# A whole network's instructions ordered by the language's timing model, with a new loading order for its input

## The chip, the core and the metric

The kernel runs on one core of a Trainium2 chip. The metric is the device time of one execution in microseconds. The kernel before takes 1856.32 us, the median of three runs between 1855.94 and 1859.72 us. The engines are called by their short names: PE multiplies matrices, DVE (VectorE) and ACT (ScalarE) work element by element on 128 partitions, POOL (GpSimd) helps out, SP issues DMAs.

## The reference

The input is 512 tokens of 1024 channels. The network has a first part of two layers and a second part of one layer. Layer A of the first part is what most of this text is about: attention in which every query attends only to the 128 best keys, chosen by a score of its own.

```python
def dsa_mixer(x, cos, sin, w_in, w_o):
    top_k = min(IDX_TOPK_MAX, L // 4)                     # 128
    q, k, v, iq, ik, iw = jnp.split(x @ w_in, A_SPLITS, axis=-1)
    ...                                                   # rotary on q, k, iq, ik
    s = einsum('bqhd,bsd->bqhs', iq_b, ik) * IDX_DIM ** -0.5
    score = einsum('bqh,bqhs->bqs', iw_b, relu(s))        # 8 index heads
    score = where(causal, score, -inf)
    _, sel = lax.top_k(score, top_k)
    p = softmax(logits of q against the selected keys)    # 16 heads, 4 kv heads
    return einsum(p, v_sel) @ w_o

def first_block(x, ...):      # layer A, then layer B
    h = layer_norm(ALPHA * h + mixer(h)); h = layer_norm(ALPHA * h + relu(h @ w_up)**2 @ w_down)

def second_block(x, c, ...):  # attention and a two-way mLSTM side by side, then a gated MLP
```

Layer B's mixer is a gated linear attention (GLA): a state per head is carried over chunks of 64 tokens; its output is normalised per head, multiplied by a gate silu(r), and projected.

## The kernel before

**Arithmetic and tiles.** Products in f32 are made from two rounded parts: `hi` (L88, on ACT) copies a tile to the type fp32r, `lo` (L85, on DVE) subtracts that copy from the original, and a product x·w becomes three PE products, hi·hi, lo·hi and hi·lo. Weights go through the same split: a piece of a weight arrives by DMA as `wr`, ACT makes `wh`, DVE makes `wl` (128x1024 at a time in most places). The 512 tokens are four tiles of 128, numbered 0 to 3. `x_tok` is the input with tokens on partitions, `xT_hi` and `xT_lo` are the transposed parts. `transpose_half` makes them: four PE transposes of 128x128 into one PSUM bank `ps_t`, then hi and lo.

**PSUM.** There are eight banks: three named `ps_a` (projections), two `ps_t` (transposes), two `ps_s` (scores), one `ps_o` (attention output).

**Layer A** (`layer_a`). It projects iq, then k and ik, and then runs the steps of the list `ORDER_A` (L22): S3 is the score of tile 3, V the projection of the values, Q0 and Q1 those of the queries (two groups of 8 heads), B3 the search of the best keys of tile 3, A30 the attention of tile 3 with head group 0, O the output projection. Tile 0 needs no search: all its causal keys are selected. A score (L508 to L526) is, for each of 8 index heads, two PE products into `ps_s`, a relu on ACT (`rl`), and one DVE instruction that adds into `sc`; tile t has 128·(t+1) keys, so `sc1` is 128x256, `sc2` 128x384, `sc3` 128x512. A search (L528 to L535) is sixteen rounds on DVE of MAX8 (the eight largest of a row), MATCH_VALUE_LOAD and MATCH_REPLACE8 (strike them out), and a last TENSOR_SCALAR (L535), which turns `sc` into the bias that the softmax adds. The attention of a tile and group (`softmax_pv`) is, for each of 8 heads, two products into `ps_s`, a DVE instruction that adds the bias and takes the row minimum (L428, `prob,mn<-ps_s,sc`), an exp on ACT (L434), a reciprocal on DVE, a normalisation on DVE or ACT, PE transposes (L443) and an ACT copy (L448), and then products with v into `ps_o`.

**GLA.** After the chunk recurrence, each head's output `gy` is copied from PSUM (L847, DVE), squared and summed (L851, ACT), a square root is taken over all sixteen sums at once (L866, ACT), then a reciprocal (L867, DVE); L883 multiplies by the gate, and `transpose_half` feeds the output projection.

**What sets the order.** The functions write instructions in program order, with pools of buffers; `urgent` gives loads and weight splits an earlier place. From this the language's scheduler makes one list per engine. An engine runs its list in order.

## Time and profile before

| | |
|---|---|
| median of three runs | 1856.32 us (1855.94 to 1859.72) |
| the profiled execution, its own time | 1859.66 us |
| its span in the profile | 1857.9 us |
| PE busy in the span | 1815.5 us |
| DVE busy | 1440.5 us |
| ACT busy | 912.3 us |

Layer A with its output projection and norm takes the first 240 us or so, the first MLP follows, the GLA lies around 600 to 800 us, the second MLP until 1165 us, the second part's mixer until about 1510 us, and its MLP to the end. In the rows below, a line such as "88.09 0.88 DVE L533 MAX8 m<-sc 128x8 f32<-128x256 f32 x2" gives the start of a run of alike instructions, its length to the end of the last one, the engine, the line in the kernel, the operation, output and inputs, and the count. The end of one instruction overlaps the start of the next by about 0.1 us, so the cadence is read from starts.

### The profile page before, as it was taken

The numbers are of one execution on the slowest core, as the hardware profiler recorded it, in microseconds if no ns is written. First come the engines' busy times: TensorE is split into PE (matmuls) and PEld (weight loads), VectorE is DVE, ScalarE is ACT, GpSimd is POOL, SyncE is SP. The second block draws the span as 40 slices with busy tenths as digits, with TensorE's granted clock in tenths as the row PEclk, the third lists the DMA queues.
The fourth block names the chain that finished last, engine by engine and source line by source line (L and its number), as shares of the span: only waits on it lengthen the run. The fifth ranks groups of instructions, "written<-read, shape, count | busy, mean of one in ns | idle before, by whom it ended". The sixth has DMA issues, their size and how long they took to land.

```text
span 1857.9 us, 26802 instructions
## 1 busy us (share of the span) xinstructions
PE 1815.5 (98%) x10564; PEld 1532.8 (83%) x10564; DVE 1440.5 (78%) x2467; ACT 912.3 (49%) x1600; POOL 19.0 (1%) x46
## 2 busy tenths in 40 slices
PE   8999999999999999999999999999999899999997
PEld 7865698988888888889888888777566689999996
DVE  5998589878678587468988777877876787788877
ACT  5568644444443544334544444445677445344334
POOL 0010000000000100000000000000000000000000
PEclk9999999999999999999999999999999999999999
DMA  4231244634324222126454323422112122333232
GB/s 143 91 68 52 67 139 158 207 117 148 103 91 134 61 69 69 68 91 188 140 180 140 113 92 111 139 73 81 46 41 69 45 91 68 114 114 114 79 104 91
DMA packets 127161, 190.80 MB, mean 103 GB/s; under 512 B 9279, under 2 KB 77835, under 8 KB 127036
## 3 DMA queue, kind: packets, MB, share of 16 engines
q1 hardware_dynamic: 126996, 189.03, 32.0%
q8 instruction: 83, 1.36, 0.3%
q14 instruction: 42, 0.34, 0.1%
q0 software_dynamic: 32, 0.07, 0.0%
q10 hardware_dynamic: 8, 0.00, 0.0%
HBM read 186.96 MB, written 2.12 MB: 102 GB/s over the span
## 4 chain that ended last, share of the span: by engine, by line
PE 92%; DVE 5%; ACT 2%; issue 0%; DMA 0%; POOL 0%; SPq 0%; DVEq 0%; ACTq 0%; POOLq 0%
PE ps_a L77 51%; PE ps_s L77 15%; PE ps_t L77 11%; PE ps_o L77 7%; PE ps_t L443 1%; PE ps_t L302 1%; PE ps_s L806 1%; PE ps_a L1275 1%; DVE wl L85 1%; PE ps_t L405 1%; PE ps_s L1241 1%; ACT prob L434 0%; PE ps_s L843 0%; PE ps_o L858 0%; ACT wh L88 0%
## 5 line engine op out<-in xcount | busy, mean ns | idle before, releaser
L88 ACT ACTIVATE wh<-wr 128x1024 fp32r<-128x1024 f32 (+2 forms) x284 | 258.6, 958 | 239.3 <-PE ps_t L77 113.3
L85 DVE TENSOR_TENSOR wl<-wr,wh 128x1024 fp32r<-128x1024 f32 (+2 forms) x284 | 304.1, 1104 | 84.6 <-ACT wh L88 55.1
L77 PE MATMUL ps_a<-wh,xT_hi 128*128 128x512 f32 (+3 forms) x536 | 205.3, 387 | 3.6 <-ACT xT_hi L88 2.2
L77 PE MATMUL ps_a<-wh,xT_lo 128*128 128x512 f32 (+3 forms) x536 | 204.3, 385 | 0.6 <-DVE xT_lo L85 0.6
L88 ACT ACTIVATE wsh<-wr 128x1024 fp32r<-128x1024 f32 x94 | 97.5, 1059 | 184.3 <-DVE wr L254 155.5
L77 PE MATMUL ps_a<-xT_hi,wh 128*128 128x256 f32 (+1 forms) x528 | 163.4, 321 | 0.9 <-DVE gtok L1097 0.5
L77 PE MATMUL ps_a<-xT_lo,wh 128*128 128x256 f32 (+1 forms) x528 | 162.7, 319 | 0.0
L77 PE MATMUL ps_a<-xT_hi,wl 128*128 128x256 f32 (+1 forms) x528 | 147.0, 319 | 0.0
L77 PE MATMUL ps_a<-wl,xT_hi 128*128 128x512 f32 (+3 forms) x536 | 143.6, 381 | 0.0
L77 PE MATMUL ps_s<-wh,hh 128*128 128x512 f32 x344 | 136.6, 397 | 0.1
L77 PE MATMUL ps_s<-wh,hl 128*128 128x512 f32 x344 | 136.7, 397 | 0.0
L77 PE MATMUL ps_a<-tl,wsh 128*128 128x256 f32 x528 | 132.1, 283 | 0.0
L77 PE MATMUL ps_a<-th,wsh 128*128 128x256 f32 x528 | 132.1, 282 | 0.0
L77 PEld LDWEIGHTS ps_a<-wh,xT_hi 128*128 128x128 f32 x536 | 101.5, 189 | 25.0 <-issue 4.5
L85 DVE TENSOR_TENSOR wsl<-wr,wsh 128x1024 fp32r<-128x1024 f32 x94 | 113.0, 1221 | 10.7 <-ACT wsh L88 10.7
L77 PEld LDWEIGHTS ps_a<-wh,xT_lo 128*128 128x128 f32 x536 | 101.5, 189 | 19.8 <-DVE xT_lo L85 1.4
L77 PE MATMUL ps_t<-wh,hl 128*128 128x512 f32 x296 | 117.4, 397 | 0.0
L77 PE MATMUL ps_t<-wh,hh 128*128 128x512 f32 x296 | 117.4, 396 | 0.0
L77 PEld LDWEIGHTS ps_a<-wl,xT_hi 128*128 128x128 f32 x536 | 95.6, 188 | 19.3 <-issue 1.6
L77 PEld LDWEIGHTS ps_a<-xT_hi,wh 128*128 128x128 f32 x528 | 100.1, 190 | 9.3 <-issue 0.8
L77 PEld LDWEIGHTS ps_a<-xT_lo,wh 128*128 128x128 f32 x528 | 100.0, 189 | 7.8 <-issue 0.8
L77 PEld LDWEIGHTS ps_a<-tl,wsh 128*128 128x128 f32 x528 | 100.3, 190 | 0.0
(437 smaller groups left out, 4122.3 us busy)
## 6 DMA issues: line engine op xcount, KB each, us to landing
wr<-in_mlp_w_up_dram SPq DMA_DIRECT2D x32, 1024.0 KB
wr<-in_mlp_w_down_dram SPq DMA_DIRECT2D x32, 1024.0 KB
mod_raw<-in_w_ada_dram SPq DMA_DIRECT2D x48, 512.0 KB
wr<-in_b_w_in_dram SPq DMA_DIRECT2D x12, 1024.0 KB
wr<-in_w_gate_dram SPq DMA_DIRECT2D x11, 1024.0 KB
wr<-in_w_up_dram SPq DMA_DIRECT2D x11, 1024.0 KB
wr<-in_w_in_dram SPq DMA_DIRECT2D x10, 1024.0 KB
wr<-in_w_down_dram SPq DMA_DIRECT2D x10, 1024.0 KB
```

The source lines that it names most:

```text
L77: self.nc.tensor.matmul(ps, lt, rt, start=first, stop=last)
L85: (eng or self.nc.vector).tensor_tensor(out, x, hi.bitcast(F32), op=ALU.subtract)
L88: self.nc.scalar.activation(out, x, AF.Copy)
L302: self.nc.tensor.transpose(ps[:, j * P : (j + 1) * P], src[:, j * P : (j + 1) * P], self.ident)
L405: nc.tensor.transpose(ps[:, j * P : (j + 1) * P], st[:, j0 + j, :], net.identr)
L443: nc.tensor.transpose(pst[:, kb * P : (kb + 1) * P], pr[:, kb * P : (kb + 1) * P], net.ident)
L806: nc.tensor.matmul(ps[:, c * 64 : c * 64 + 64], x[:, c * C : (c + 1) * C], xv[:, c * m : (c + 1) * m, 1, :], start=True, stop=True)
L1241: nc.tensor.matmul(ps, qk[:, 4 + h, a * P : (a + 1) * P], qk[:, h, :], start=True, stop=True)
L1275: nc.tensor.matmul(o, ws[a][:, b * P : (b + 1) * P], v1[:, a, h, 0:129], start=n == 0, stop=n == len(as_) - 1)
```

## The change

The changed kernel computes the same. Four things differ.

1. The whole body stands in a block that the language's scheduler orders by its detailed timing model: instead of the program order with its urgent places alone, each engine's list is made from times that a model of the engines gives.
2. `load_x` loads both halves of the first weight (the iq projection) and the input in another order, in half tiles, and for tiles 1 to 3 the first half's hi parts are rounded by DVE (`copy=nc.vector.tensor_copy`) instead of ACT.
3. The first projection goes over its three tiles as one group instead of two and one (`group=3`).
4. `warm` writes nine PE products of the identity with itself into a `ps_s` bank that nobody reads, ahead of everything else on PE.

```diff
--- before.py
+++ after.py
@@ -48,10 +48,18 @@
         self.xl = self.cp.tile([P, KB, S], F32R, name="xT_lo")
         self.ident = self.cp.tile([P, P], F32, name="ident")
         make_identity(nc, self.ident)
+        self.epst = {}
+        self.nurgent = 0
+        self.warm(5)
         self.identr = self.cp.tile([P, P], F32R, name="identr")
         nc.vector.tensor_copy(self.identr, self.ident)
-        self.epst = {}
-        self.nurgent = 0
+
+    def warm(self, n):
+
+        with self.urgent():
+            ps = self.bank("s")
+            for _ in range(n):
+                self.nc.tensor.matmul(ps[:, :P], self.ident, self.ident, start=True, stop=True)
 
     def new_xt(self):
         self.xt = self.cp.tile([P, NT, D], F32, tag="xt", name="x_tok")
@@ -143,13 +151,13 @@
         for _ in self.proj_steps(*args, **kw):
             pass
 
-    def proj_steps(self, ah, al, chunks, n, evac, tiles=range(NT), serial=False, tags="a"):
+    def proj_steps(self, ah, al, chunks, n, evac, tiles=range(NT), serial=False, tags="a", group=2):
 
 
         tiles = list(tiles)
         nck = len(chunks)
         got = {}
-        for t0 in ([[t] for t in tiles] if serial else [tiles] if nck == 1 else [tiles[i : i + 2] for i in range(0, len(tiles), 2)]):
+        for t0 in ([[t] for t in tiles] if serial else [tiles] if nck == 1 else [tiles[i : i + group] for i in range(0, len(tiles), group)]):
             ps = {}
             for ci in range(nck):
                 if ci not in got:
@@ -295,14 +303,15 @@
         return eo
 
 
-    def transpose_half(self, src, oh, ol, t, half):
+    def transpose_half(self, src, oh, ol, t, half, copy=None):
 
         ps = self.bank()
         for j in range(4):
             self.nc.tensor.transpose(ps[:, j * P : (j + 1) * P], src[:, j * P : (j + 1) * P], self.ident)
         pv = ps.rearrange("p (k n) -> p k n", k=4)
         sl = (slice(None), slice(4 * half, 4 * half + 4), slice(t * P, (t + 1) * P))
-        self.split(oh[sl], ol[sl], pv)
+        (copy or self.hi)(oh[sl], pv)
+        self.lo(ol[sl], pv, oh[sl])
 
     def bcast_row(self, dst, row):
 
@@ -488,7 +497,8 @@
                     transpose_stack(net, sv, 8, lambda j0, m: dst[:, h0 + j0 : h0 + j0 + m, (t - tofs) * P : (t - tofs + 1) * P])
                 return f
 
-            net.proj_tok(*xk, [lambda: (*first, [0, 1, 2, 3]), net.wtok(w_in, (1536, 512))[1]], 512, ev_heads(iqT, 1, 0, None), tiles=range(1, NT))
+            net.proj_tok(*xk, [lambda: (*first[0], [0, 1, 2, 3]), lambda: (*net.wsplit(first[1], 4, 512), [4, 5, 6, 7])], 512,
+                         ev_heads(iqT, 1, 0, None), tiles=range(1, NT), group=3)
             def ev_k(t, ps):
 
                 nc.vector.tensor_scalar(iws[:, t, :], ps[:, 320:328], float(np.float32(8.0 ** -0.5)), None, op0=ALU.mult)
@@ -1411,25 +1421,37 @@
 
 def load_x(net, src, w=None):
 
+
     nc = net.nc
-    order = (1, 2, 3, 0)
-    n = w.shape[1] if w is not None else 0
+    half = lambda t, h: (net.xt[:, t, h * 512 : h * 512 + 512], net.xh, net.xl, t, h)
+
+    def xd(t, h):
+        nc.sync.dma_start(net.xt[:, t, h * 512 : h * 512 + 512], src[t * P : (t + 1) * P, h * 512 : h * 512 + 512])
+    if w is None:
+        for t in range(NT):
+            for h in range(2):
+                xd(t, h)
+                net.transpose_half(*half(t, h))
+        return None
+    n = w.shape[1]
     with net.urgent():
-        if w is not None:
-            raw = net.wp.tile([P, 2048], F32, tag="raw", name="wr")
-        for i, t in enumerate(order):
-            for h in range(2):
-                sl = slice(h * 512, h * 512 + 512)
-                nc.sync.dma_start(net.xt[:, t, sl], src[t * P : (t + 1) * P, sl])
-                if i == 0 and w is not None:
-                    for k in (2 * h, 2 * h + 1):
-                        nc.sync.dma_start(raw[:, k * n : (k + 1) * n], w[k * P : (k + 1) * P, :])
-    if w is not None:
-        first = net.wsplit(raw, 4, n, pieces=4)
-    for t in order:
-        for h in range(2):
-            net.transpose_half(net.xt[:, t, h * 512 : (h + 1) * 512], net.xh, net.xl, t, h)
-    return first if w is not None else None
+        raw = [net.wp.tile([P, 2048], F32, tag="raw", name="wr") for _ in range(2)]
+
+        def wd(i, k0, k1):
+            nc.sync.dma_start(raw[i].rearrange("p (k n) -> p k n", k=4)[:, k0:k1],
+                              w[i * 512 + k0 * P : i * 512 + k1 * P, :].rearrange("(k p) n -> p k n", p=P))
+        for f, *args in ((xd, 1, 0), (wd, 0, 0, 1), (wd, 0, 1, 2), (xd, 2, 0), (wd, 0, 2, 3), (wd, 0, 3, 4), (xd, 3, 0),
+                         (wd, 1, 0, 2), (xd, 1, 1), (wd, 1, 2, 4), (xd, 2, 1), (xd, 3, 1), (xd, 0, 0), (xd, 0, 1)):
+            f(*args)
+
+        net.transpose_half(*half(1, 0), copy=nc.vector.tensor_copy)
+        net.warm(4)
+        first = net.wsplit(raw[0], 4, n, pieces=4)
+        for t in (2, 3):
+            net.transpose_half(*half(t, 0), copy=nc.vector.tensor_copy)
+    for t, h in ((1, 1), (2, 1), (3, 1), (0, 0), (0, 1)):
+        net.transpose_half(*half(t, h))
+    return first, raw[1]
 
 
 def store_x(net, dst):
@@ -1468,12 +1490,17 @@
 STAGES = ["ln1", "mlp1", "ln2", "mlp2", "out"]
 
 
+def tile_net(tc: tile.TileContext, ins, out, first=0, last=4):
+    with tc.block(schedule_with_timeline_sim=True):
+        tile_all(tc, ins, out, first, last)
+
+
 @with_exitstack
-def tile_net(ctx: ExitStack, tc: tile.TileContext, ins, out, first=0, last=4):
+def tile_all(ctx: ExitStack, tc: tile.TileContext, ins, out, first, last):
     net = Net(ctx, tc, ins, out)
     dp = ctx.enter_context(tc.tile_pool(name="dr_mod", bufs=1, space=bass.MemoryType.DRAM))
     net.mod = dp.tile([6, D], F32, name="mod")
-    fw = load_x(net, ins["x"][0], ins["a_w_in"][0][0:512, 1536:2048] if first == 0 else None)
+    fw = load_x(net, ins["x"][0], ins["a_w_in"][0][:, 1536:2048] if first == 0 else None)
     if first == 4:
         with tc.tile_pool(name="ada", bufs=1) as ap:
             for e in ada(net):
```

With the block, rows move on all engines. Three places follow. In the first, DVE's list in layer A; `sc1`, `sc2`, `sc3` are the scores of tiles 1, 2, 3, `caus` the causal mask that tile 0 uses. Before, around the end of tile 1's search:

```order
L534 MATCH_REPLACE sc2_607<-m8_2_1664,sc2_607 128x384
L533 MAX m8_1_1034<-sc1_827 128x8
L438 TENSOR_SCALAR prob_1141<-prob_1141,rcp_1145 128x128
L534 MATCH_REPLACE sc1_827<-m8_1_1034,sc1_827 128x256
L436 RECIPROCAL rcp_1159<-sum_1157 128x1
L436 RECIPROCAL rcp_1173<-sum_1171 128x1
L535 TENSOR_SCALAR sc1_827<-sc1_827 128x256
L438 TENSOR_SCALAR prob_1169<-prob_1169,rcp_1173 128x128
L436 RECIPROCAL rcp_1187<-sum_1185 128x1
L428 ISA prob_1198,mn_1197<-ps_s_1194,caus_162 128x128
L428 ISA mn_1197 128x1
```

After, around the end of tile 1's search (the same code stands eight to ten lines lower, L428 is L437 and L535 is L545):

```order
L543 MAX m8_1_1044<-sc1_840 128x8
L544 MATCH_REPLACE sc1_840<-m8_1_1044,sc1_840 128x256
L543 MAX m8_1_1047<-sc1_840 128x8
L544 MATCH_REPLACE sc1_840<-m8_1_1047,sc1_840 128x256
L545 TENSOR_SCALAR sc1_840<-sc1_840 128x256
L437 ISA prob_1273,mn_1272<-ps_s_1269,sc1_840 128x256
L437 ISA mn_1272 128x1
L437 ISA prob_1288,mn_1287<-ps_s_1284,sc1_840 128x256
```

Before, tile 1's search ends while tile 2 has three of its sixteen rounds and tile 3 all sixteen still to come, and these stand further down between the softmax instructions. After, all 48 rounds stand ahead of the first softmax row that uses a searched bias; tile 1's search is the last to end.

The second place is PE's list at the first score (`ps_s<-iq`). The 128x256 products are those of the value projection. Before:

```order
L77 MATMUL ps_a<-wh,xT_lo 128x256
L77 MATMUL ps_a<-wl,xT_hi 128x256
L405 MATMUL ps_t<-identr,kst 128x128 x6
L77 MATMUL ps_a<-wl,xT_hi 128x256
L405 MATMUL ps_t<-identr,kst 128x128 x4
L77 MATMUL ps_s<-iq 128x384 x4
L77 MATMUL ps_a<-wl,xT_hi 128x256 x2
L77 MATMUL ps_a<-wh,xT_hi 128x256
```

After:

```order
L85 MATMUL ps_a<-wh,xT_lo 128x256
L85 MATMUL ps_a<-wh,xT_hi 128x256
L85 MATMUL ps_a<-wh,xT_lo 128x256
L414 MATMUL ps_t<-identr,kst 128x128 x4
L85 MATMUL ps_s<-iq 128x384 x4
L414 MATMUL ps_t<-identr,kst 128x128 x2
L85 MATMUL ps_a<-wh,xT_hi 128x256
L85 MATMUL ps_a<-wh,xT_lo 128x256
L85 MATMUL ps_a<-wl,xT_hi 128x256 x4
```

Counted from the start of the lists, ten products of 128x256 stand ahead of the first score before, and 66 after; nothing else of that work differs but the nine unread products.

The third place is PE's list at the end of the GLA recurrence; `state,qe` is its last kind of product, and the 128x512 products behind it are those of the gate's projection. Before:

```order
L858 MATMUL ps_o<-gv,kdt 128x256
L845 MATMUL ps_s<-state_7162,qe 128x256
L843 MATMUL ps_s<-gv,attnT 128x256
L845 MATMUL ps_s<-state_7163,qe 128x256
L77 MATMUL ps_a<-wh,xT_hi 128x512
L77 MATMUL ps_a<-wh,xT_lo 128x512
L77 MATMUL ps_a<-wl,xT_hi 128x512 x4
L77 MATMUL ps_a<-wh,xT_hi 128x512
L77 MATMUL ps_a<-wh,xT_lo 128x512
```

After:

```order
L855 MATMUL ps_s<-state_7174,qe 128x256
L868 MATMUL ps_o<-gv,kdt 128x256
L855 MATMUL ps_s<-state_7175,qe 128x256
L853 MATMUL ps_s<-gv,attnT 128x256
L855 MATMUL ps_s<-state_7176,qe 128x256
L310 MATMUL ps_t<-ident,gy 128x128 x4
L85 MATMUL ps_a<-wh,xT_hi 128x512
L85 MATMUL ps_a<-wh,xT_lo 128x512
```

Before, projection products follow the last state product and the transposes of `gy` come over a hundred rows later; after, the transposes of `gy` are the next row.

## Rows read from the trace of the kernel before

**Rows 1.** The profile's page, busy engines, and the engines' shares of the closing chain

```profile
PE 1815.5 (98%) x10564; PEld 1532.8 (83%) x10564; DVE 1440.5 (78%) x2467; ACT 912.3 (49%) x1600; POOL 19.0 (1%) x46
...
PE 92%; DVE 5%; ACT 2%; issue 0%; DMA 0%; POOL 0%; SPq 0%; DVEq 0%; ACTq 0%; POOLq 0%
```

**Rows 2.** The table by stretch: start:end, length, busy us of each engine (instructions), PEclk

```profile
1100.00:1500.00 400.00, 382.52 (x1930) 295.23 (x1929) 303.91 (x590) 220.01 (x444) 2.93 (x14) 0.98 0.24 74
1800.00:1858.00 58.00, 47.52 (x287) 41.61 (x285) 43.61 (x68) 23.31 (x42) 0.00 (x0) 0.93 0.25 91
```

**Rows 3.** The timeline at the start, PE

```profile
3.58 1.09 PE L302 MATMUL ps_t<-ident,x_tok 128*128 128x128 f32 x4 [3.58 <-DMA x_tok<-in_x_dram]
...
8.91 0.79 PE L77 MATMUL ps_a<-wh,xT_hi 128*128 128x512 f32 x1 [1.47 <-ACT xT_hi L88]
...
17.04 0.39 PE L77 MATMUL ps_a<-wh,xT_lo 128*128 128x512 f32 x1
...
17.27 0.40 PE L77 MATMUL ps_a<-wh,xT_hi 128*128 128x512 f32 x1
```

**Rows 4.** PE's timeline shortly before the first score

```profile
50.10 0.28 PE L77 MATMUL ps_a<-wh,xT_hi 128*128 128x256 f32 x1
50.22 0.28 PE L77 MATMUL ps_a<-wh,xT_lo 128*128 128x256 f32 x1
```

**Rows 5.** DVE's timeline in layer A

```profile
53.87 0.42 DVE L523 TENSOR_SCALAR sc<-rl,iws 128x384 f32<-128x384 f32 x1
...
88.09 0.88 DVE L533 MAX8 m<-sc 128x8 f32<-128x256 f32 x2
...
89.80 0.88 DVE L533 MAX8 m<-sc 128x8 f32<-128x256 f32 x2
...
92.30 2.34 DVE L85 TENSOR_TENSOR wl<-wr,wh 128x1024 fp32r<-128x1024 f32 x2
...
105.08 0.27 DVE L428 CUSTOM_DVE_ANT_0 prob<-ps_s,caus 128x128 f32<-128x128 f32 x1
...
110.09 0.28 DVE L535 TENSOR_SCALAR sc<-sc 128x256 f32<-128x256 f32 x1
...
110.97 1.15 DVE L533 MAX8 m<-sc 128x8 f32<-128x384 f32 x2
...
114.11 0.67 DVE L534 MATCH_REPLACE8 sc<-m,sc 128x512 f32<-128x512 f32 x1
```

**Rows 6.** The table by stretch in layer A

```profile
60.00:110.00 50.00, 49.41 (x268) 40.18 (x267) 49.26 (x149) 26.81 (x54) 0.00 (x0) 1.00 0.33 85
...
145.00:215.00 70.00, 65.57 (x327) 40.42 (x326) 53.99 (x192) 61.40 (x165) 0.00 (x0) 1.00 0.15 45
```

**Rows 7.** ACT's timeline, first exp of tile 1

```profile
115.65 0.50 ACT L434 ACTIVATE prob<-prob,mn 128x256 f32<-128x256 f32 x1
```

**Rows 8.** ACT's timeline, last weight pieces and last attention copy

```profile
207.90 2.01 ACT L88 ACTIVATE wh<-wr 128x1024 fp32r<-128x1024 f32 x2
...
216.58 0.60 ACT L448 ACTIVATE pt<-ps_t 128x512 f32<-128x512 f32 x1 [0.74 <-PE ps_t L443]
```

**Rows 9.** The chain of waits at the attention's end: start, length, what

```profile
217.48 3.58 PE ps_o L77 x14
```

**Rows 10.** The timeline behind the GLA recurrence

```profile
751.10 0.69 DVE L847 COPY gy<-ps_s 128x512 f32<-128x512 f32 x1 [0.82 <-PE ps_s L845]
...
752.81 1.28 ACT L866 ACT_TABLE_LOAD   x1
...
754.11 0.31 ACT L866 ACTIVATE ssq<-ssq,c 128x16 f32<-128x16 f32 x1
...
754.45 0.25 DVE L867 RECIPROCAL ssq<-ssq 128x16 f32<-128x16 f32 x1 [2.66 <-ACT ssq L866]
...
759.40 0.87 DVE L883 SCALAR_TENSOR_TENSOR gy<-gy,ssq,r 128x256 f32<-128x256 f32 x2
```

**Rows 11.** The table by stretch where the granted clock is lowest in the mixer

```profile
1265.00:1275.00 10.00, 9.11 (x32) 6.91 (x33) 5.00 (x27) 5.60 (x21) 0.02 (x1) 0.66 0.63 206
```

## The prediction

> **What bounds the kernel.** I read the page first. PE is busy for 1815.5 of 1857.9 us and holds 92% of the chain that ended last [rows 1]. The two lists hold the same PE work but for the nine unread products, so a new order can win back at most the 42 us in which PE stands, and it can lose wherever PE is made to wait. The table by stretch says where PE stands: 17.5 of 400 us in the second mixer and 10.5 in the last 58 [rows 2], the rest at the start and in layer A. Layer A is the place to look at, because there PE is not the tightest engine. From 60 to 110 us DVE is busy for 49.3 of 50 us, and from 145 to 215 us ACT for 61.4 of 70 (88%) [rows 6]. First DVE searches, then ACT does the softmax; the kernel before starts the second while the first still runs. Tile 1's search ends at 110.1 us [rows 5], its first exp stands at 115.65 [rows 7], and the remaining search rounds go on between the softmax instructions.
>
> The sum is a difference. It is made on the profiled execution, 1859.66 us by its own clock (span 1857.9), which is 3.3 us or 0.2% above the median of 1856.32. I add it to the median; on the profiled execution it would be 3.3 us more.
>
> **Step 1, the start.** Four f32 transposes of 128x128 took 1.09 us [rows 3], so nine unread products of that size take about 2.5 us. They need only the identity and come while PE waits for the first input tile, which arrives at 3.6 us: cost 0, at most 0.5 if they end late; a PE that waits for nothing hides them. The first weight product took 0.79 us at 8.91, one at 17.04 took 0.39, and there starts are 0.23 apart [rows 3]: the same instruction at the lower and at the higher of PE's two levels, 1.2 and 2.4 GHz, after a PE that had mostly waited for input. In the list of before, 13 such products and 24 transposes stand in the 8.1 us between. At full speed they cost 13 x 0.23 + 24 x 0.135 (half of the 0.27 above) = 6.2. So 1.9 us is the most that a full-speed start saves, and 0 the least, since PE stands again between the unread products and the first weight product, which cannot be much earlier: the hi part that it needs now stands on DVE behind the third `wl`. I take 1.5 less. The Trainium skill, "TensorE: Matmul & The Clock Gate", Part 1, says that the throttled state is the default and activity releases it; by that alone the whole 1.9 would be saved, by the pause in PE's work nothing.
>
> **Step 2, the first score.** 56 more products of 128x256 now stand ahead of it on PE. Starts of such products are 0.12 us apart [rows 4], so that is 6.7 us. They are moved, not added, but DVE's search waits for the scores. DVE's first score instruction, at 53.87 before [rows 5], comes at 53.9 + 6.7 - 1.5 = 59.1 us.
>
> **Step 3, the search.** Before, from the first score instruction to the end of tile 1's bias, DVE needs 53.87 to 110.09 and 0.28 more: 56.5 us [rows 5]. After, the same stretch of DVE's list holds everything that it held and the following besides.
> - 16 rounds of tile 3. One 256 round and one 384 round together take 89.80 - 88.09 = 1.71 us. A strike-out on 512 takes 0.67 [rows 5]; with a MAX8 of about the same length, the short load and the overlaps of 0.1 off, a 512 round is 1.25. That gives 20.0 us.
> - 3 more rounds of tile 2 at about 1.0: 3.0 us.
> - 4 more `wl` of 128x1024 at half of 2.34, less the overlap [rows 5]: 4.5 us.
> - some twenty short instructions (four more heads of tile 0, two finals, `hst`, `oa`) at about 0.2, since the nearest one takes 0.27 with its overlap [rows 5]: 4.4 us.
>
> That is 31.9 us more. In addition, the scores of tile 2 are now spread out between PE's projections, so DVE will wait between them; by PE's list (products counted at the spacings above) they span about 15 us, in which DVE's list holds about 11 us of work. I add 3 (0 to 5). Tile 1's bias is then ready at 59.1 + 56.5 + 31.9 + 3 = 150.5 us, 40 later than before. With the start at its better bound and no waits it is 147, with its worse bound and 5 us of waits 154.
>
> The first softmax row of tile 1 stands right behind the last search row on DVE, and DVE runs its list in order. Behind it wait ACT's exp of every head of tiles 1 to 3; on PE, the two `ps_s` banks fill with tile 1's products, and the transposes of its probabilities and all that follows wait too. PE has by its list some 110 us of work ahead of that point, so it stands for about 30 us. This is the wait that the change adds.
>
> **Step 4, the attention after it.** Before, from the first exp of tile 1 at 115.65 to the end of the last attention copy at 217.2 [rows 7, 8] there are 101.5 us, of which ACT worked about 86 (61.4 of it in one stretch of 70 us [rows 6]). After, ACT's list from that exp on is the same but for four weight pieces of 1.0 each [rows 8] and a few evacuations that went ahead: 79.5 us. DVE no longer searches there, and PE has some 44 projection products fewer in between. At ACT's 88% the stretch takes 90 us, at 100% 79.5, at the share of before 94. I take 90, because the softmax chain of one head (DVE, ACT, DVE, PE, ACT) stays, and because 88% is what ACT reached where the search no longer competed much. The last copy then ends at 150.9 + 90 = 241 us, 23.7 later. Behind the last attention product [rows 9], 4 us less PE work is left than before, as more of the output projection's and queries' products have gone ahead. Layer A: +19.7 us. The bounds are 147 + 79.5 and 154 + 94, so +5 to +27.
>
> **Step 5, the GLA.** The transposes of `gy` now stand right behind the last state product. Before, projection products stood there. The chain from that product is in the trace: copy of the last `gy` at 751.10, squares, a table load at 752.81, the square root at 754.11, the reciprocal at 754.45 for 0.25, one multiplication by the gate (half of 0.87) [rows 10]. So the transposes can start at about 755.2, and PE stands for 4.2 us. The cover that goes is the gate's projection. The recurrence itself also has no projection between its steps now; I add 1. GLA: +5, with 0 and 9 as bounds.
>
> **Step 6, the rest.** Both MLPs keep PE busy through, and the lists hold the same work: 0. In the second mixer projections move ahead of the attention, which is then left with fewer fillers; PE's idle 17.5 us [rows 2] can shrink or grow: 0, with 10 either way. The last 58 us are nearly the same list: 0.
>
> Sum: +19.7 + 5 = +24.7, so about 1880 us. The group of three tiles and the DVE roundings are in steps 1 and 2; they get no cost of their own, since DVE, like PE, waits for the first input there.
>
> **Rivals.**
> - ACT runs without a gap after the search, and DVE does not wait for the scores. For it: DVE is freed of 21 us of rounds there. Against it: ACT never reached more than 88% over 70 us [rows 6]. Layer A +5 to +8, GLA +2: 1865 us.
> - Faster than before: the second mixer gives more than layer A takes. Place: 1100 to 1500 us, where 17.5 us of PE idle lie [rows 2] with DVE at 76% and ACT at 55%, so that an order with better times could fill them. Price: up to 15 of the 17.5. It decides once layer A and the GLA together lose less than that; with layer A at +5 and the GLA at 0 it gives 1846 us. Against it: layer A's loss rests on DVE's list alone.
> - The new order costs and gains nothing that can be told: a search that ends late is absorbed, because PE has other products to do meanwhile. It has 110 us of them and would need 140. 1856 us.
> - The wait slows PE afterwards. In the mixer there is a stretch with a granted clock of 0.66, between the levels of 1.2 and 2.4 GHz, though PE was busy for 9.1 of 10 us [rows 11]. If PE comes out of 30 us of waiting at the lower level and falls back to it between the heads, its 70 us of work in step 4 stretch by some 10: 1890 us. The Trainium skill, "TensorE: Matmul & The Clock Gate", Part 1, says that an idle array is throttled again, which speaks for this one; that the start was slow and the clock then rose agrees, but no run here shows layer A's clock after a long wait.
>
> **How the numbers follow.** Forecast 0.60 (its own range 1867 to 1891), the dense ACT 0.13, the slow clock 0.07, faster 0.13, no change 0.07. The predicted time is 1880 us. The range that should hold it 8 times in 10 goes from 1856, which takes in the dense ACT, to 1895, which takes in the slow clock. A measurement can tell about 0.2% (3.7 us) from no change. Slower by more: 0.79; within: 0.07; faster: 0.14.
>
> **What would show it.** In the profile of the changed kernel: the last MAX8 near 150 us and no softmax instruction with a searched bias ahead of it; PE idle for 20 to 35 us somewhere between 115 and 152; the last attention copy near 241; ACT busy near 88% after the search; PE idle for 4 to 5 us behind the GLA recurrence. If the search ends by 130, or PE does not stand, steps 2 and 3 are wrong. If the search ends late and the end of the attention moves by less than 10 us, step 4 is. If both hold and the total does not move, step 6 is.

## The result and the profile after

The changed kernel takes 1959.48 us (median of 4 runs, 1956.34 to 1963.93), the kernel before 1858.02 (4 runs, 1855.94 to 1861.68): a ratio of 1.0546 [1.0517, 1.0574]. It is slower by 101 us, where 24 were forecast, and lies outside the range. The profiled execution of the changed kernel took 1959.83 us, its span 1958.1.

From here on the kernel is cut into six stages. Layer A goes from the start to the first down product of the first MLP, so its norm and the first up products are in it. MLP0 ends with its last down product, GLA and MLP1 are cut alike, the mixer ends where VectorE first evaluates the second part's MLP, and the FFN is the rest.

The page of the changed kernel, busy engines and closing chain, answers to [rows 1]:

```profile
PE 1849.4 (94%) x10582; PEld 1563.6 (80%) x10582; DVE 1442.0 (74%) x2470; ACT 914.7 (47%) x1602; POOL 20.9 (1%) x46
...
PE 80%; DVE 12%; ACT 4%; DMA 2%; issue 1%; SPq 0%; POOL 0%; DVEq 0%; ACTq 0%; POOLq 0%
```

DVE and ACT are busy as long as before. PE is busy 34 us longer, though it got only the nine unread products, which took 4.2 us; its share of the chain fell from 92 to 80%. Next, the table by stretch for three stages (columns as in [rows 2]), before and then after:

```profile
0.00:287.10 287.10, 273.62 (x1498) 211.13 (x1499) 222.69 (x626) 178.61 (x411) 7.46 (x24) 1.00 0.33 101
600.20:880.20 280.00, 279.48 (x1558) 236.44 (x1557) 193.48 (x335) 119.45 (x216) 8.63 (x8) 1.00 0.29 93
1192.60:1567.20 374.60, 356.88 (x1861) 276.18 (x1860) 290.46 (x569) 212.04 (x438) 2.93 (x14) 0.98 0.21 64
```

```profile
0.00:329.10 329.10, 288.56 (x1516) 223.97 (x1517) 227.59 (x630) 176.94 (x408) 7.93 (x24) 0.94 0.30 89
642.00:945.90 303.90, 290.26 (x1567) 244.82 (x1566) 194.52 (x337) 128.80 (x225) 8.63 (x8) 0.96 0.27 87
1256.60:1666.60 410.00, 369.18 (x1877) 289.23 (x1876) 291.64 (x569) 211.44 (x439) 4.36 (x14) 0.94 0.19 58
```

Layer A is 42.0 us longer, the GLA 23.9, the mixer 35.4: all of the loss. Length less PE's busy time is what PE stands, that is, the time in which no product runs: 27.1, 13.1 and 23.1 us more than before, 63 in all. The rest, 14.9, 10.8 and 12.3, is more busy time. Not all of it is the same products taking longer: 4.2 us in layer A are the nine unread ones, and the GLA and the mixer hold 9 and 16 products more than before, which the new order moved there. Over the whole kernel, where nothing can move in or out, PE stands 66 us more and is busy some 30 us more for the same work, at a lower granted clock. In e_block below, which has no unread products, it is 67 and 26.5 us. So much of PE's standing is followed by slower products.

The GLA shows how. PE's timeline at the wait that step 5 had forecast from [rows 10], and the table behind it:

```profile
834.11 0.59 PE L855 MATMUL ps_s<-state,qe 128*128 128x256 f32 x2
838.92 1.12 PE L310 MATMUL ps_t<-ident,gy 128*128 128x128 f32 x4 [4.21 <-DVE gy L893]
...
840.61 0.63 PE L85 MATMUL ps_a<-wh,xT_lo 128*128 128x512 f32 x1
841.04 0.63 PE L85 MATMUL ps_a<-wh,xT_hi 128*128 128x512 f32 x1
...
844.71 0.39 PE L85 MATMUL ps_a<-wh,xT_hi 128*128 128x512 f32 x1
```

```profile
838.90:842.00 3.10, 3.08 (x9) 2.21 (x10) 3.10 (x8) 2.63 (x5) 0.00 (x0) 0.50 0.07 26
842.00:846.00 4.00, 4.00 (x15) 3.17 (x14) 3.83 (x11) 0.00 (x0) 0.00 (x0) 0.75 0.00 0
```

The wait is 4.21 us long. Behind it the granted clock is 0.50 (1.2 of 2.4 GHz), products start 0.43 us apart instead of 0.23, and the higher level is back some five us later.

At the start, PE's timeline answers to [rows 3]:

```profile
1.47 4.21 PE L62 MATMUL ps_s<-ident 128*128 128x128 f32 x18 [1.47 <-POOL ident masks.py:199]
5.48 1.06 PE L310 MATMUL ps_t<-ident,x_tok 128*128 128x128 f32 x4
...
9.71 0.47 PE L85 MATMUL ps_a<-wh,xT_hi 128*128 128x512 f32 x1 [1.93 <-DVE pos_f L351]
```

In layer A tile 1's search ends last of the three. VectorE's timeline, and PE's first product behind it:

```profile
148.40 0.08 DVE L544 MATCH_VALUE_LOAD sc<-m,sc 128x8 f32 x1
148.47 0.40 DVE L544 MATCH_REPLACE8 sc<-m,sc 128x256 f32<-128x256 f32 x1
148.80 1.00 DVE L543 MAX8 m<-sc 128x8 f32<-128x512 f32 x2
149.72 0.07 DVE L544 MATCH_VALUE_LOAD sc<-m,sc 128x8 f32 x1
149.78 0.67 DVE L544 MATCH_REPLACE8 sc<-m,sc 128x512 f32<-128x512 f32 x1
...
156.01 0.29 DVE L545 TENSOR_SCALAR sc<-sc 128x256 f32<-128x256 f32 x1
```

```profile
156.82 0.58 PE L85 MATMUL ps_s<-kTh,qT 128*128 128x256 f32 x1 [13.09 <-DVE mn L437]
```

Rounds of 256 (tile 1) and of 512 (tile 3) take turns. The last instruction of all three searches starts at 156.0, earlier than the 172.7 of before; but tile 1's, for which the attention waits, comes 46 us later than in [rows 5].

The table by stretch, from 115 us to the end of that wait and from there to the last attention copy (answers to [rows 6]):

```profile
115.00:156.80 41.80, 20.39 (x65) 13.09 (x64) 41.42 (x139) 11.34 (x35) 1.51 (x4) 0.69 0.23 51
156.80:252.20 95.40, 87.54 (x426) 55.74 (x426) 54.21 (x210) 78.39 (x217) 1.79 (x4) 0.98 0.10 34
```

At the norm between layer A and MLP0, PE's timeline and VectorE's:

```profile
289.88 1.97 PE L310 MATMUL ps_t<-ident,x_tok 128*128 128x128 f32 x8 [5.28 <-DVE xT_lo L93]
```

```profile
285.07 1.22 DVE L93 TENSOR_TENSOR wl<-wr,wh 128x1024 fp32r<-128x1024 f32 x1
...
286.87 2.35 DVE L93 TENSOR_TENSOR wl<-wr,wh 128x1024 fp32r<-128x1024 f32 x2
289.14 1.28 DVE L93 TENSOR_TENSOR xT_lo<-ps_t,xT_hi 128x512 fp32r<-128x512 f32 x2
```

The output projection's products all went ahead of the norm. While VectorE norms and splits weights, PE has nothing left. In the mixer the waits are spread. Of PE's the longest groups are these (us in total, times, longest), and behind them what three of them were before:

```profile
PE ps_s L85 <- ACT prob L443: 7.5, 6, 2.6
PE ps_t L310 <- DVE xT_lo L93: 6.6, 3, 3.3
PE ps_t L310 <- DVE rows_tl L991: 5.3, 1, 5.3
PE ps_a L1285 <- DVE wexp L1274: 4.2, 3, 3.3
```

```profile
PE ps_a L1275 <- DVE wexp L1264: 3.5, 3, 1.6
PE ps_t L302 <- DVE rows_tl L981: 3.4, 2, 2.7
PE ps_s L77 <- ACT prob L434: 1.2, 3, 0.9
```

### The profile page after: what moved, and what is told of

Its sections match the earlier page's. It is cut to its first block, busy times and chain, and to the rows that moved or that the text cites. A ratio compares the mean times of both kernels' runs of the same rounds, so it can differ in the third digit from the quotient of the medians.

```text
span 1958.1 us, 26779 instructions
## 1 busy us (share of the span) xinstructions
PE 1849.4 (94%) x10582; PEld 1563.6 (80%) x10582; DVE 1442.0 (74%) x2470; ACT 914.7 (47%) x1602; POOL 20.9 (1%) x46
## 4 chain that ended last, share of the span: by engine, by line
PE 80%; DVE 12%; ACT 4%; DMA 2%; issue 1%; SPq 0%; POOL 0%; DVEq 0%; ACTq 0%; POOLq 0%
PE ps_a L85 45%; PE ps_s L85 13%; PE ps_t L85 10%; PE ps_o L85 6%; DVE wl L93 2%; DMA mod_raw<-in_w_ada_dram 1%; PE ps_s L816 1%; PE ps_a L1285 1%; ACT prob L443 1%; DVE sc L544 1%; PE ps_t L310 1%; PE ps_t L452 1%; DVE x_tok L335 1%; DVE m L543 1%; DVE x_tok L336 1%
## 5 line engine op out<-in xcount | busy, mean ns | idle before, releaser
L85 PEld LDWEIGHTS ps_a<-th,wsh 128*128 128x128 f32 x528 | 100.3, 190 | 3.0 <-ACT wsh L96 2.3
```

What stands on the lines that cost most here:

```text
L85: self.nc.tensor.matmul(ps, lt, rt, start=first, stop=last)
```

## The experiments

Each ratio is to the kernel before, timed beside it (1858.7 to 1860.1 us). The stages, in us, from the profiled executions:

| run | median | layer A | MLP0 | GLA | MLP1 | mixer | FFN |
|---|---|---|---|---|---|---|---|
| before | | 287.1 | 313.1 | 280.0 | 312.4 | 374.6 | 290.7 |
| changed | 1959.5 | 329.1 | 312.9 | 303.9 | 310.7 | 410.0 | 291.5 |
| e_edits | 1864.0 | 291.8 | 313.8 | 279.9 | 311.7 | 375.3 | 290.6 |
| e_block | 1954.1 | 328.4 | 311.7 | 300.9 | 310.6 | 408.6 | 291.6 |
| e_s1first | 1942.0 | 312.8 | 311.7 | 300.8 | 311.0 | 409.7 | 291.5 |
| e_rest | 1925.6 | 290.9 | 312.4 | 308.7 | 311.6 | 407.5 | 291.6 |
| p_pe | 1945.7 | 312.7 | 321.5 | 284.2 | 329.7 | 393.0 | 300.0 |
| p_dve | 2030.9 | 340.8 | 315.3 | 329.1 | 314.4 | 438.1 | 291.3 |
| p_pedve | 1893.9 | 294.5 | 317.6 | 281.8 | 317.1 | 378.0 | 303.4 |
| p_pesearch | 1937.8 | 302.8 | 323.2 | 284.6 | 331.3 | 394.1 | 299.9 |
| p_stagesb | 1884.0 | 287.6 | 319.0 | 289.2 | 318.2 | 379.6 | 290.7 |
| e_fill | 1956.8 | 331.5 | 312.0 | 299.8 | 310.6 | 409.7 | 291.4 |

**Which part of the change: e_edits (the edits without the block), e_block (the block without the edits).**

```diff
-    with tc.block(schedule_with_timeline_sim=True):
-        tile_all(tc, ins, out, first, last)
+    tile_all(tc, ins, out, first, last)
```

> The changed kernel without the timing-model block; the new loading, the group of three tiles, the DVE roundings and the nine unread products stay. Theory 1 (the order made by the timing model causes the whole loss): 1854 to 1859 us, tile 1's search ends near 110 us, PE idle in the span near 42 us. Rival (the edits at the start or the group of three cause part of it): 1875 us or more, with the loss in the first 240 us.

> The kernel before, with only the timing-model block around its body. Theory 1: 1950 to 1965 us, tile 1's search is the last of the three and ends near 155 us, the first product of the first MLP's second half comes some 42 us later than before. Rival (the edits cause part): under 1935 us.

Measured: e_edits 1863.98 us, ratio 1.0027 [1.0018, 1.0036]; e_block 1954.08, 1.0509 [1.0491, 1.0527]. They add up: 5.3 and 95.4 us of 101. The block's order is nearly all of the loss. The 5.3 of the edits were not expected: e_edits misses its range, with 4.7 us lost in layer A, where the rival had placed a loss, though one of at least 16 us. In e_edits VectorE's list and PE's first weight product read:

```profile
11.54 1.22 DVE L93 TENSOR_TENSOR wl<-wr,wh 128x1024 fp32r<-128x1024 f32 x1 [1.61 <-ACT wh L96]
12.69 1.28 DVE L313 CAST xT_hi<-ps_t 128x512 fp32r<-128x512 f32 x2
```

```profile
13.52 0.77 PE L85 MATMUL ps_a<-wh,xT_hi 128*128 128x512 f32 x1 [5.85 <-DVE xT_hi L313]
```

The roundings, now VectorE's, queue behind a weight part that has to wait for the second half of the weights; the product that came at 8.91 [rows 3] comes at 13.52.

**The late search alone: e_s1first** (the changed kernel, tile 1 scored and searched first)

```diff
-ORDER_A = "S2 V S3 V S1 Q0 B1 Q0 A00
+ORDER_A = "S1 B1 S2 V S3 V Q0 Q0 A00
```

> The changed kernel, with tile 1's score and search written first in layer A's step list (S1 B1 S2 V S3 V Q0 in place of S2 V S3 V S1 Q0 B1). The block stays. Theory 2 (layer A loses because DVE finishes tile 1's search last): tile 1's search ends between 95 and 120 us, no PE wait of over 5 us on the first softmax, layer A's share of the loss (42 us at the first product of the first MLP's second half, 329 against 287 us) falls to 5 to 12, the total is 1920 to 1932 us. Rival (the output projection, the reload of x and the norm behind the attention make most of layer A's loss): total above 1945 us.

Measured: 1942.01, 1.0443 [1.0428, 1.0459]. The search of tile 1 ends at 104.5, earlier than before the change, and the 13-us wait is gone; yet layer A gets back only 16 of its 42 us. That is a miss: 25.7 us of loss stay where 5 to 12 were expected, and the total lies in neither range. The new step order also moves projections on PE, so the 16 is the worth of this order and not of the search alone; the 5.3-us wait at the norm stays. The forecast's own mechanism is real and less than half of that stage.

**Does each stage lose for itself: e_rest** (layer A and MLP0 outside the block)

```diff
+    stage(0)
+    stage(1)
+    with tc.block(schedule_with_timeline_sim=True):
+        for s in range(2, last + 1):
+            stage(s)
```

> The changed kernel with the block around layer B, the second MLP and the second part only; layer A and the first MLP are ordered without the timing model. Theory 3 (each stage loses for itself, layer A 42, the GLA 23, the mixer 35, the MLPs nothing): 1912 to 1922 us, the first product of the first MLP's second half at 285 to 289 us. Rival (stages hand their delays and their slow clock on, or the mixer's loss follows from what comes before): under 1900 or over 1935 us.

Measured: 1925.62, 1.0359 [1.0343, 1.0374]. The GLA (308.7) and the mixer (407.5) lose as much behind an undisturbed layer A, so their loss is not a delay handed on from there. The total is 3.6 us above the expected range; the GLA takes 4.8 longer than in the changed kernel, with waits of 2.9 and 3.8 us for `x_tok` at the norm where the block begins.

**Whose list: p_pe, p_dve, p_pedve.** Theory 1 was that PE's list alone is the cause, theory 2 that VectorE's is. The instructions of the changed kernel are the same with and without the model, so a list can be copied from one to the other, by an edge from each instruction to the one ahead of it:

```diff
     with tc.block(schedule_with_timeline_sim=True):
         tile_all(tc, ins, out, first, last)
+        pin(tc)
...
+            if prev is not None:
+                tc.add_manual_dep(i, prev.name, mybir.DependencyInfo(mybir.DependencyClass.NoSync, mybir.DependencyReason.DATA), reason="order")
+            prev = i
```

> The changed kernel with its block and its timing model, but TensorE's 10,206 products and transposes are queued in the order that a plain block (without the model) gives the same program; the model still orders VectorE, ScalarE and the DMA queues. Theory 1 (the model puts products of projections onto TensorE as soon as they are ready, so that the recurrence, the norms, the softmax and the mixer find none left to fill their waits): nearly all of the block's 95 us goes, 1864 to 1885 us; the 4.2-us wait at the gy transposes is gone and MLP0's first hidden product starts by 295 us (329 in the changed kernel, 291.8 with the edits alone). Theory 2 (it is VectorE's order: the search of tile 1 behind other work, roundings behind weight splits): over 1930 us, since VectorE's order is still the model's.

> The changed kernel with its block and its timing model, but 2,294 of VectorE's instructions are queued in the order that a plain block gives the same program; the model still orders TensorE. Theory 1 (TensorE's order): 1930 to 1960 us, with PE idle of some 40 us left in the layer before MLP0 or in the mixer. Theory 2 (VectorE's order): 1864 to 1885 us, search of tile 1 ended by 120 us.

> The changed kernel with block and model, but TensorE and VectorE both in the plain block's order; only ScalarE, GpSimd and the DMA queues stay with the model. By theory 1 and by theory 2 alike 1860 to 1868 us (the edits without the model measured 1864). Over 1880 us: ScalarE's order or the DMA issues carry a part of the loss that neither theory names.

Measured: p_pe 1945.67, 1.0467 [1.0451, 1.0484]; p_dve 2030.89, 1.0921 [1.0905, 1.0938]; p_pedve 1893.85, 1.0184 [1.0169, 1.0199]. Both theories fell as stated: neither list alone brings the time back, and the old VectorE list under the model's PE list is 71 us worse than the changed kernel. Only both together return layer A, the GLA and the mixer to within 2 to 3 us of e_edits. The traces agree on the GLA: in p_pe the 4.2-us wait at gy and the 5.3-us wait at the norm of layer A are gone, in p_dve the wait at gy stays, at 4.7. The table read stage by stage says more. In layer A, the GLA and the mixer, the old PE list is worth 16, 20 and 17 us beside the model's VectorE list, and 46, 47 and 60 beside the old one. The old VectorE list costs 12, 25 and 28 beside the model's PE list, and is worth 18, 2 and 15 beside the old one. So PE's list is the larger part in the mixer and nearly the whole of the GLA (303.9 to 284.2 by itself); in layer A the two weigh about the same (16 and then 18) when PE's is put back first. VectorE's list counts once PE's is right. In the MLPs and the FFN the mixture is worse than either whole: p_pe loses 8.6, 19.0 and 8.5 us there against the changed kernel. p_pedve, too, was expected at 1860 to 1868 and stays 30 us above e_edits: 3.8, 5.4 and 12.8 us of that lie in the MLPs and the FFN, 7.3 in the other three stages. As the expectation had said of a time over 1880, the orders of ScalarE and the DMA queues, still the model's there, carry a part in this mixture that neither theory names; which instructions these are was not taken apart. The pinning itself costs nothing that can be told: e_fill, pinned to the changed kernel's own order, takes 1956.8.

**What of VectorE's list, in layer A: p_pesearch** (p_pe, and 96 search instructions in the old order)

```diff
 ORDERS = {
     'PE': (
...
+    'DVE': (
...
```

> The kernel of p_pe (TensorE in the plain block's order, the rest by the model; 1945.7 us, layer A 312.7 us, tile 1's search ends last of the three, at 137.6 us) with 96 instructions of VectorE more queued in the plain block's order: the rounds of the three searches, so that tile 1's search is done before most of tile 2's and all but a few of tile 3's. If the search is what the model's VectorE order still costs in layer A once TensorE's is restored: search of tile 1 ended by 112 us, layer A 294 to 300 us (294.5 with all of VectorE pinned), the whole 1926 to 1934 us. Rival (softmax steps, roundings and weight splits stand wrongly too): layer A over 304 us.

Measured: 1937.77, 1.0424 [1.0406, 1.0442]; tile 1's search ends at 116.2 and layer A at 302.8, between the two expectations; the total misses both. The search is 9.9 of the 18.2 us by which p_pe's layer A exceeds p_pedve's. The other 8.3 lie with the rest of VectorE's list, which was not taken apart.

**Can the model keep the MLPs: p_stagesb** (the kernel before, all lists pinned but the two MLPs')

```diff
+    free = range(tc.marks[1], tc.marks[2]), range(tc.marks[3], tc.marks[4])
+    ins = {int(i.name[2:]): i for k, i in enumerate(tc.nc.cur_bb.bb.instructions) if not any(k in f for f in free)}
```

> The kernel before, without the three edits, in one block with the timing model, but the instructions of all engines in layer A, layer B and the second part (mixer and FFN) are queued in the order of the kernel before; the model orders the two MLPs alone. By the stages of the earlier runs (MLP0 313.1 before and 311.7 to 312.9 under the model, MLP1 312.4 and 310.6 to 310.7) the model gains 0.5 to 3 us in the MLPs and loses nothing elsewhere: 1855 to 1858 us, a ratio of 0.998 to 1.000. If the model's loss does not sit in the three stages with chains but comes with the block itself (its buffers, its waits), this stays above 1880 us.

Measured: 1884.04, 1.0126 [1.0109, 1.0143]. A miss, in the rival's range (above 1880): the MLPs lose 5.9 and 5.8 us instead of gaining, and the GLA and the mixer, though pinned, 9.2 and 5.0. The table by stretch shows two places, one inside MLP0 and one at the norm behind it, where MLP0 ends and the GLA begins:

```profile
305.00:315.00 10.00, 6.75 (x41) 5.29 (x39) 10.00 (x14) 6.16 (x10) 0.00 (x0) 1.00 0.00 0
605.00:615.00 10.00, 6.39 (x29) 5.17 (x28) 10.00 (x18) 1.88 (x4) 0.00 (x0) 0.74 0.35 106
```

VectorE is full and PE stands for over 3 of 10 us: in the first stretch 4.2 us for a weight piece that ScalarE splits (`wsh`), in the second 1.83, 0.54 and 1.25 us for `xT_lo` of the norm, as behind MLP0 in the changed kernel. So the small gain of the MLPs in the table (1.7 us of MLP1 in the changed kernel) did not come with the model's order of the MLPs alone. A piece of one order need not keep its time inside another.

**The edits' 5.3 us: e_startpin** (the edits without the model, the first twelve VectorE instructions in the changed kernel's order)

```diff
+START = (118, 120, 122, 108, 124, 130, 109, 131, 274, 137, 276, 138)
```

> The edits without the timing model (measured 1864, 5.3 us over the kernel before), with one thing more: VectorE's first twelve instructions are queued in the changed kernel's order, the roundings of x between the weight parts instead of behind the part that waits for the second half of the weights. If that order is what the 5.3 us were (first weight product at 13.5 us instead of 8.9): first weight product by 10 us and 1858 to 1861 us, no slower than the kernel before by more than 2 us. Rival (the three-tile group or the nine unread products cost it): 1863 to 1865 us.

Measured: 1861.14, 1.0010 [1.0000, 1.0019]. The first weight product comes at 10.06 instead of 13.52, and 3.3 of the 5.3 us are back: most of it was the roundings' place. The other 2.0, with the unread products and the group of three tiles in them, were not taken apart.

**The clock: e_fill** (the changed kernel in its own order on every engine, with unread products in two of PE's waits)

```diff
+    pso = net.bank("o"); bias is not None and (t, kofs) == (1, 0) and fill(net, pso, 40)
...
+        ps = self.bank(); fill(self, ps, n)
```

> The changed kernel with every engine's instructions queued in its own order, and unread products of the identity added at two of TensorE's waits: 40 before the first score product of tile 1's attention (wait of 13.1 us) and 16 before the first gy transposes (wait of 4.2 us). They use a bank that the next products overwrite. If the lower clock after a wait comes from TensorE standing idle: behind the gy transposes the products run at 0.23 us from the first on (0.43 us for the first eight in the changed kernel), and the layer up to MLP1's first hidden product is some 2.8 us shorter than 303.9 us; behind the 13-us wait the products of the attention run at the higher level, but VectorE and ScalarE feed them there, so that little of it is won back. Rival (the products behind the wait are slow for their own sake, as fresh operands or a bank that is read): 0.43 us again. The whole time: 1953 to 1960 us.

`fill` issues that many products of the identity. One run, 1956.81 us. PE's timeline at the gy transposes (one such product counts twice):

```profile
833.46 0.59 PE L855 MATMUL ps_s<-state,qe 128*128 128x256 f32 x2
833.89 3.73 PE L1496 MATMUL ps_t<-ident 128*128 128x128 f32 x32
838.26 0.83 PE L310 MATMUL ps_t<-ident,gy 128*128 128x128 f32 x4 [0.64 <-DVE gy L893]
...
839.70 0.40 PE L85 MATMUL ps_a<-wh,xT_lo 128*128 128x512 f32 x1
839.93 0.39 PE L85 MATMUL ps_a<-wh,xT_hi 128*128 128x512 f32 x1
...
842.27 0.40 PE L85 MATMUL ps_a<-wh,xT_hi 128*128 128x512 f32 x1
```

The same products, for the same operands, now start 0.23 us apart from the first on. From the last recurrence product to the one at 842.27 it is 8.8 us, in the changed kernel 10.6 (834.11 to 844.71). So the clock was at most 1.8 us of this wait's price; 2.8 were expected. From the first gy transpose to that product it is 4.0, 5.8 in the changed kernel and in e_block, and 4.9 in e_s1first, so 0.9 to 1.8 by the run. Products behind gy start 0.43 us apart in all five other traces that have this wait (the changed kernel, e_block, e_s1first, e_rest and p_dve), and only here not. The whole GLA is 4.1 us shorter than in the changed kernel, but e_block and e_s1first, without the products, have 300.9 and 300.8: the rest goes with the norm behind MLP0, where the granted clock over 10 us was 0.70 in the changed kernel and 1.00 in these three runs, behind the same waits. In layer A the 40 products took 9.09 us and left 5.26 of standing; behind these the attention's products started 0.21 us apart as in the changed kernel, at the lower level (0.12 is the higher [rows 4]). So at gy the unread products kept the clock up; in layer A, with the end of the wait uncovered, they did not.

**The same on the kernel before: b_fill** (its own order, nine unread products ahead of one pair of kst transposes)

```diff
-                                        lambda j0, m: dst[:, j0 : j0 + m, tsl])
+                                        lambda j0, m: dst[:, j0 : j0 + m, tsl], idle=9 * (t == 1 and i == 0))
```

> The kernel before in its own order, with nine unread products of the identity added at one of TensorE's waits in the mixer: before the transposes of kst of tile 1, where TensorE stands 2.32 us and the next 13 products run at 0.43 us and more instead of 0.23 us. If the clock theory holds, the products behind run at 0.23 us and the stretch to 1273 us is some 3 us shorter: 1855.5 to 1857.5 us against 1859 (ratio 0.998 to 0.9995), a version that beats both kernels if the gain reaches the end. Rival (a later wait for VectorE or ScalarE takes it back): 1858 to 1860 us with the stretch shorter all the same.

PE's timeline there, before and with the nine products:

```profile
1265.35 0.36 PE L405 MATMUL ps_t<-identr,kst 128*128 128x128 f32 x2 [2.32 <-ACT kst L1090]
...
1268.48 0.63 PE L77 MATMUL ps_a<-xT_hi,wh 128*128 128x512 f32 x1
1268.91 0.63 PE L77 MATMUL ps_a<-xT_lo,wh 128*128 128x512 f32 x1
```

```profile
1265.46 2.17 PE L1474 MATMUL ps_t<-ident 128*128 128x128 f32 x18
1267.93 0.37 PE L405 MATMUL ps_t<-identr,kst 128*128 128x128 f32 x2 [0.30 <-ACT kst L1090]
...
1270.16 0.39 PE L77 MATMUL ps_a<-xT_hi,wh 128*128 128x512 f32 x1
1270.38 0.39 PE L77 MATMUL ps_a<-xT_lo,wh 128*128 128x512 f32 x1
```

Behind the nine products the clock stays up, and the stretch from the last product ahead of the wait to the same product behind it takes 9.25 us instead of 12.16, 2.9 less, as forecast. Measured: 1856.98 us, 0.9988 [0.9979, 0.9997]: 0.12% faster than the kernel before, less than the 0.2% that one comparison can tell well. How much of this is the stretch is not settled, since the two profiles differ in other places too (from 1325 to 1350 us the granted clock is 0.93 before and 1.00 here).

## Why the prediction was wrong

The side was right; the size was a quarter. Step by step:

- **Step 1, the start: -1.5.** The gain did not come; it was about nothing. For the nine products "cost 0, at most 0.5 if they end late" was too low: they end at 5.68, so the first x transposes start at 5.48 instead of 3.58 [rows 3]. Such a product stands in the trace as two records (x18 for nine), so four transposes of 1.09 us were no measure for it: nine took 4.21 us, not 2.5. The first weight product comes at 9.71 instead of 8.91, not for that but because the rounding stands behind the third `wl` on DVE, as step 1 had seen. At the first product of the value projection PE is 0.75 us ahead (49.11 against 49.86), but with 6 transposes of `kst` done instead of 20. Without the block the edits lose 5.3 us.
- **Step 2, first score 59.1.** It came at 60.31.
- **Step 3, search of tile 1 ends at 150.5.** It ended at 156.3, 96.0 us after the first score instruction instead of 91.4. The term that was too small is DVE's own waiting: DVE stood for 8.6 us there where 3 (0 to 5) were put. PE stood for 21.4 of the 41.8 us from 115 on, at the low end of the 20 to 35. The mechanism was right, and e_s1first prices it at 16 to 17.5 us.
- **Step 4, 90 us of attention, layer A +19.7.** The first exp of tile 1 came at 156.8, 5.9 us later than forecast, and from there to the last copy at 252.2 the attention took 95.4, 5.4 longer, with ACT busy for 82% and not 88%. Worse, behind it "4 us less PE work" was counted as 4 us less time; in fact the stretch from there to MLP0 grew by 7.0, to 76.9 us. PE has 15 products fewer there but is busy as long as before (69.8 against 69.9) and stands for 7.1 us, 5.28 of them at the norm, since the output projection that had gone ahead had covered it. The 5.9, the 5.4 and these 11 are the 22 us between +19.7 and +42.
- **Step 5, the GLA +5.** The wait at gy is 4.21 us, forecast 4.2. But it is followed by slow products, and the norms on both sides of the stage add waits of 1.83, 0.54 and 1.13 us at 644 to 648 and of 0.83 and 2.36 at 903 to 907: +23.9. That the recurrence had lost its products was seen, that the norms had lost theirs was not.
- **Step 6, the rest 0.** This is the step that failed most: the mixer lost 35.4 us. That "projections move ahead of the attention, which is then left with fewer fillers" was written down and then priced at 0 with 10 either way. PE stands 23.1 us more there; the old PE list alone brings 17.0 of the 35.4 back, with the old VectorE list 32.0. Both MLPs were right at 0.
- **The clock rival at 10 us and a chance of 0.07.** It is not a rival but a surcharge on much of the standing: about 30 us over the whole kernel, for 66 us of standing. The Trainium skill, "TensorE: Matmul & The Clock Gate", Part 1, says an idle array is throttled again; e_fill shows it at gy, at 0.9 to 1.8 us.

In one sentence: two stages were priced by the one wait that was found in the list and the mixer at nothing, while the order takes the fillers away in all three. The cause that the runs show is PE's list (products issued as early as they can be, ahead of the work that needs cover) together with VectorE's (tile 1's search last). That the products moved ahead are the fillers that lack is read from the lists and the waits; the runs show whose lists it is. Not isolated are which of PE's moves in the mixer cost what, the last 8 us of VectorE's in layer A, and the 30 us by which p_pedve stays above e_edits.

## What to carry to other kernels

When an order puts the same products earlier, ask for each place they leave what covers that place now: the norms, the recurrence, the softmax; price each, and add something for PE's clock behind the waits: 0.40 (e_block) to 0.45 (the changed kernel) of the added standing here, as an average and not wait by wait. Two engines' lists are one schedule: copying one engine's list back, or one stage's, can be worse than either whole. And a search or a projection that ends earlier in total may still end later where it is waited for.

## What the runs showed of the hardware

- With more standing PE was busy longer for the same work: 30 us for 66 us of standing in the changed kernel, 26.5 for 67 in e_block.
- The same wait is not always followed by the lower level. Behind the kst wait of 2.31 or 2.32 us the products kept 0.43 us apart until 7.5 us behind its end in the kernel before and until 4.9 us in e_startpin, in the same order. At the norm behind MLP0, behind waits of 1.83, 0.5 and 1.1 to 1.5 us, the granted clock over 10 us was 0.70 in the changed kernel and 1.00 in e_block, e_s1first and e_fill.
- Nine products of 128x128 on an engine that had done nothing yet took 4.21 us, 0.47 each; sixteen of them behind the recurrence took 3.73, 0.23 each.
